# First MLP product: weight sums on DVE, each block loaded once for them, conv steps and stores at fixed distances

## The chip, the cores and the metric

The kernel runs on one core of a Trainium2 chip. The metric is the device time of one execution in microseconds; the median of three runs stands for a kernel. The engines are TensorE (PE in the profile; its weight loads are PEld), VectorE (DVE), ScalarE (ACT), GpSimd (POOL) and SyncE (SP). Each executes its own instructions in a fixed order and waits on semaphores. SP issues most transfers, POOL a few; both do so in the order of their queues.

## What is computed

One step of a hybrid decoder layer: a state-space and pooling mixer, attention over a memory, and a gated MLP with a causal width-3 convolution between its up-projection and its gate. The change concerns the MLP alone. For the 1024 prompt tokens and 8 samples of 4 tokens, 1056 in all, with D = 1024 and D_FF = 2816:

```python
h = rmsnorm(x, norm_ffn)
u = h @ w_up                                        # 1024 -> 2*2816
u, ffn_new = causal_dwconv(ffn_buf, u, ffn_conv_w, ffn_conv_b)   # width 3
g, val = jnp.split(u, [D_FF], axis=-1)
x = x + (jax.nn.silu(g) * val) @ w_down             # 2816 -> 1024
```

The convolution of each sample starts from two stored rows of its history, and the last two rows of each sequence are an output (ffn_new). The prompt starts from zeros.

## The kernel before

All arrays are held transposed: channels on the 128 partitions, the 1056 tokens along the free dimension. Every f32 operand of a product is split in two f32r parts: hi is a rounded copy made by ACT, lo is the rest, made by DVE as raw minus hi. A product is then three matmuls per block (hi x hi, lo x hi, hi x lo). Weight blocks are 128 x 512 (four 128 x 128 blocks, 256 KB): `wr` or `ws` is the raw tile, `wh` and `wl` the split ones. There are 3 buffers of wr, wh and wl each and 6 of ws.

The order of the program is written out by hand. `steps` is the list of weight steps; `prep()` does the next step and then issues what `issue` has for that step (loads, a few steps ahead). `next_unit()` runs `prep()` until two split blocks are ready and hands out the first, so that the split of the next block is written in front of the matmuls of this one. `tick()` is called inside the products: it runs hooks whose count is up (`later(n, fn)`: n ticks later) and advances background generators (`background(gen, every)`: one step of the generator each `every` ticks). The order in an engine's queue can still differ from the program's: the framework orders instructions that do not depend on each other, except where `strict` or `force` ties an engine to the program's order (line 92), and in the MLP neither is set.

The first MLP product is done by a seven-product scheme for 2 x 2 blocks. The blocks of one pair j (a gate block of 128 channels and its value block, 22 pairs) are a11, a12, a21, a22 (two output blocks by two halves of the contraction), the tokens are halved in lh and rh of 528. The seven weight operands are a11, a21 (replaced by a11 - a21), s2 = a11 - s1, a22, s1 = a21 + a22, a12, and s4 = s2 + a12; their products are called b11, t3, t2, t4, t1, b21 and b22. A product (`product`, line 1510) is 24 matmuls of 264 columns, in two PSUM banks, with four ticks. For 14 of the pairs, `EARLY`, b21 is made ahead of all pairs (`up_rh`) and put to scratch memory `m2`; for these pairs b11 goes to a tile q, and an accumulating load on POOL adds m2 to it.

`paired(j, names)` (line 228) sets up the weight steps of a pair. Its sums come about in two ways. s2 and a11 - a21 are made by DVE in the step `adds`. The other two are made by accumulating transfers on POOL (`more`): a21 is loaded a second time into a tile s1 and a22 is added to it on its way from memory; a12 is loaded into a tile s4 and s2 is added to it, from SBUF to SBUF. So a pair takes four loads of ws tiles and one of wr on SP, one more of wr for b21 (in the pair, or ahead for the EARLY ones), and two accumulating transfers on POOL.

`up(j)` (line 1541) makes the products of pair j. PSUM is evicted by ACT (b11, t3, t2, b22: 264 columns each half) or DVE with an addition (t4, t1, b21), into r0 and r1, the raw rows of the two blocks. The order of the products is b11 of j, b22 of j-1, then t3, t2, t4, t1 and, if j is not EARLY, b21 of j. `ends(s)` (line 1546) puts the history in front of the rows: POOL sets two columns to zero, copies the samples' history and, for the output, the last two rows; ACT copies the samples' 32 new columns behind their history. It is called right behind the product. `rest()` (line 1555) is the background generator that does the convolution: ACT scales and adds the bias, DVE does two multiply-adds (128 x 1104) per block, ACT the Silu of the gate, DVE the product of gate and value. Its steps go on every 1.3 ticks (`CONV_EVERY`), after 4 steps of delay per block (`REST_LAG`). Then DVE makes the operand sums of the second product (one for j < 11, three for j >= 11) and SP stores all to scratch memory `g1` or `g2`; the store is written right behind each result.

The second MLP product is a seven-product scheme too (`DN_ORDER`, line 1746 on). Its operands come back through `x_ops` (line 1643), a background generator: `fetch()` loads 264 KB from g1 or g2 into a q tile (4 buffers), and `parts` splits it in hi (ACT) and lo (DVE). Two loads are made at its start, and one more after every split, so that loads are two items ahead. It starts at pair 19 with one item, goes on in the last pair as `limit` allows, every 4 ticks (`X_EVERY_UP`), and in the second product every 3.6 ticks (`X_EVERY_DN`). `load_acc` loads the eight residual tiles that the second product adds to, one after each weight unit that does not begin a block, but not in the first block of b11.

Of the kernel before, what the change touches and what calls it, by code (L numbers as in the profile page):

```python
# [7 lines left out]
F32 = mybir.dt.float32  # L8
# [37 lines left out]
CONV_EVERY = 1.3  # L46
REST_LAG = 4
# [4 lines left out]
X_EVERY_DN = 3.6  # L52
SUMS_EVERY = 1.6
X_EVERY_UP = 4
# [24 lines left out]
def body(ctx, tc, A):  # L79
# [53 lines left out]
    ones = cst[:, 128:256]  # L133

# [93 lines left out]
    def paired(j, names):  # L228
        q, ids = {}, {}

        def get(n):
            load(ids[n])
            q[n] = raws[ids[n]][0]

        def more(n, x):
            load(ids[n])
            G.dma_start(raws[ids[n]][0], x() if callable(x) else x, accum_op=ALU.add)

        def adds():
            for n in ("a11", "a21", "s1"):  # L240
                get(n)
            q["s2"] = stmp()
            V.tensor_tensor(q["s2"], q["a11"], q["s1"], op=ALU.subtract)
            V.tensor_tensor(q["a21"], q["a11"], q["a21"], op=ALU.subtract)

        def one(n):
            if n not in q:
                get(n)
            wsplit(q[n], 512)

        n0 = len(steps) - 1
        steps.insert(n0, adds)
        for n, m, off, alloc in (("s1", "a21", -7, stmp), ("a11", "a11", -4, wtile), ("a21", "a21", -4, stmp),
                                 ("s4", "a12", 0, stmp), ("a22", "a22", 5, stmp)):
            ids[n] = source(up_part(j, m), n0, -off, alloc)
        for n, x, off in (("s1", up_part(j, "a22"), -5), ("s4", lambda: q["s2"], 1)):
            issue.setdefault(n0 + off, []).append(lambda n=n, x=x: more(n, x))
        if j:
            steps.insert(n0 + 1, lambda: one("a11"))
            names = names[1:]  # L260
        for n in names:
            if n == "a12":
                plains([up_part(j, "a12")])
            else:
                steps.append(lambda n=n: one(n))
# [1275 lines left out]
    def up(j):  # L1541
# [4 lines left out]
        def ends(s):  # L1546
            raw = raws2[s]
            ext = raw[:, 1058:1106].rearrange("p (b t) -> p b t", b=8)
            G.memset(raw[:, 0:2], 0.0)
            G.tensor_copy(ext[:, :, 0:2], fh[:, s])  # L1550
            S.activation(ext[:, :, 2:6], raw[:, 1026:1058].rearrange("p (b t) -> p b t", b=8), AF.Copy)
            G.tensor_copy(st[:, s, 0:2], raw[:, 1024:1026])
            G.tensor_copy(st[:, s, 2:18].rearrange("p (b t) -> p b t", b=8), ext[:, :, 4:6])

        def rest():
            for s in range(2):
                while len(done) <= s:
                    yield
                for _ in range(REST_LAG):
                    yield  # L1560
                raw, f = raws2[s], 2 * j + s
                c = cv[s] = utile()
                S.activation(c[:, :1104], raw[:, 2:1106], AF.Identity, scale=pc("fw", 3 * f + 2), bias=pc("fb", f))
                yield
                if s and j >= NH:
                    kept = stile()
                    dma(kept[:, :T], scr["g1"][j - NH][:, TH:])
                for q in range(2):
                    V.scalar_tensor_tensor(c[:, :1104], raw[:, q:q + 1104], pc("fw", 3 * f + q), c[:, :1104],
                                           op0=ALU.mult, op1=ALU.add)  # L1570
                    yield
                if s == 0:
                    S.activation(c[:, :1104], c[:, :1104], AF.Silu)
                    yield
# [4 lines left out]
            p = j % NH  # L1579
            yield  # L1580
            t = u[:, :TH]
            if j < NH:
                dma(scr["g1"][p][:, :T], g[:, :T])
                V.tensor_tensor(t, g[:, rh], g[:, lh], op=ALU.subtract)
                dma(scr["g1"][p][:, T:], t)
            else:
                dma(scr["g2"][p][:, :T], g[:, :T])
                V.tensor_tensor(kept[:, lh], g[:, rh], kept[:, lh], op=ALU.subtract)
                yield
                V.tensor_tensor(kept[:, rh], kept[:, rh], g[:, rh], op=ALU.subtract)  # L1590
                yield
                V.tensor_tensor(t, kept[:, rh], g[:, lh], op=ALU.add)
                dma(scr["g2"][p][:, T:2 * T], kept[:, :T])
                dma(scr["g2"][p][:, 2 * T:], t)
                stored.append(p)
# [18 lines left out]
        ends(0)  # L1614
        background(rest(), CONV_EVERY, bgs2)
# [10 lines left out]
        ends(1)  # L1626
        done.append(1)
        dma(A["o_ffn"][j], st)
# [12 lines left out]
    limit = [0]  # L1641

    def x_ops():
# [3 lines left out]
        def fetch():  # L1647
            if left:
                n, p = left.popleft()
                while n not in ("b11", "t1") and len(stored) <= p:  # L1650
                    next(bgs2[0][0])
# [5 lines left out]
        fetch()  # L1657
        fetch()
        for i, (n, p) in enumerate(todo):
            while i >= limit[0]:  # L1660
                yield
# [3 lines left out]
            fetch()  # L1665
# [23 lines left out]
    pace(X_EVERY_DN)  # L1689

# [56 lines left out]
    for i, name in enumerate(DN_ORDER):  # L1747
# [4 lines left out]
        for m, (c0, c1) in dn_units(name):  # L1752
# [15 lines left out]
            if c0 and len(acc) < 8 and (name, m) != ("b11", 0):  # L1768
# [217 lines left out]
```

## Time and profile before

| | us |
|---|---|
| runs | 1680.94, 1685.15, 1678.08 |
| median | 1680.94 |
| the profiled execution | 1682.67 |
| its span, first to last instruction | 1680.9 |
| first MLP product (b21 of the early pairs, then the pairs) | about 960 to 1440 in the span |
| second MLP product | about 1440 to 1675 |
| mean granted clock of TensorE | 0.997 of full speed |

A row of a group reads: line, engine, operation, what it writes from what it reads, its shapes, count, then busy time and the mean of one in ns, then the idle time of the engine just in front of these instructions and what ended it. In this kernel all instructions are recorded by one helper, so every row says L91, and groups are told apart by their tiles: wl<-ws,wh is the lo part of a weight block, ws<-wr,ws a sum of weight blocks, t<-t,par a conv step, t<-mb,t an eviction with addition, q<-scr_g an operand load of the second product. A row of a timeline has start, duration and, in brackets, the idle time before it with its releaser. In the table by stretches each engine has its busy time and count of instructions; PEclk is the granted clock of TensorE, 1.00 for full speed.

### The profile page before, as it was taken

How to read it: one execution, taken by the hardware profiler on the slowest of the kernel's cores; microseconds unless marked ns; L12 is line 12 of the kernel's file. 1: busy time of each engine (PE TensorE's matmuls, PEld its weight loads, DVE VectorE, ACT ScalarE, POOL GpSimd, SP SyncE). 2: the span in 40 equal slices, each digit the busy share in tenths (PEclk: the TensorE clock that was granted, in tenths of full speed). 3: DMA queues.
4: the chain of work that ended last, by engine and by line, in shares of the span. 5: the costliest groups of instructions: out<-in, count | busy, mean ns of one | idle time of the engine just before them, and what ended most of it. 6: DMA issues, size and time to landing. Idle time of an engine off the chain costs nothing. (4 is left out here: it accounts for less than half of the span.)

```text
span 1680.9 us, 30585 instructions
## 1 busy us (share of the span) xinstructions
PE 1642.8 (98%) x11808; PEld 1559.3 (93%) x11808; DVE 1180.9 (70%) x1999; ACT 784.4 (47%) x1402; POOL 138.7 (8%) x315
## 2 busy tenths in 40 slices
PE   9999999999999999999999999999999999999998
PEld 8899999899989889999878999999999989999997
DVE  6766768688679576654755896777777878776665
ACT  6565643444514343223533665555544545454451
POOL 0110000001000000000000002232122222100000
PEclk9999999999999999999999999999999999999999
DMA  6243354544696678853666756666566577896542
GB/s 219 85 160 87 66 134 105 111 87 107 224 314 230 192 252 304 301 165 105 233 226 192 228 182 170 177 167 180 145 167 199 168 205 218 284 302 203 159 139 103
DMA packets 187569, 306.57 MB, mean 182 GB/s; under 512 B 43920, under 2 KB 81296, under 8 KB 187424
## 3 DMA queue, kind: packets, MB, share of 16 engines
q1 hardware_dynamic: 178928, 289.04, 54.6%
q0 software_dynamic: 8496, 15.59, 5.6%
q8 instruction: 92, 1.51, 0.4%
q14 instruction: 53, 0.43, 0.1%
HBM read 221.26 MB, written 77.53 MB: 178 GB/s over the span
## 5 line engine op out<-in xcount | busy, mean ns | idle before, releaser
L91 PE MATMUL mb<-s,wh 128*128 128x264 f32 (+4 forms) x4800 | 908.3, 295 | 6.8 <-ACT wh L91 4.7
L91 PEld LDWEIGHTS mb<-s,wh 128*128 128x128 f32 x4800 | 759.5, 189 | 15.1 <-ACT wh L91 5.8
L91 PE MATMUL mb<-s,wl 128*128 128x264 f32 (+4 forms) x2400 | 667.5, 296 | 13.7 <-DVE wl L91 13.3
L91 PEld LDWEIGHTS mb<-s,wl 128*128 128x128 f32 x2400 | 445.8, 189 | 23.6 <-DVE wl L91 20.5
L91 ACT ACTIVATE wh<-wr 128x512 fp32r<-128x512 f32 (+1 forms) x298 | 184.7, 620 | 385.1 <-PE mb L91 177.2
L91 PE MATMUL mm<-s,wh 128*128 128x352 f32 x1728 | 340.9, 330 | 1.5 <-DVE s L91 1.5
L91 PEld LDWEIGHTS mm<-s,wh 128*128 128x128 f32 x1728 | 284.6, 188 | 7.9 <-DVE s L91 2.6
L91 DVE TENSOR_TENSOR wl<-wr,wh 128x512 fp32r<-128x512 f32 (+1 forms) x298 | 201.4, 677 | 109.9 <-ACT wh L91 107.4
L91 PE MATMUL mm<-s,wl 128*128 128x352 f32 x864 | 187.7, 324 | 0.0
L91 DVE SCALAR_TENSOR_TENSOR t<-t,par 128x1104 f32<-128x1104 f32 (+1 forms) x124 | 168.2, 1366 | 26.5 <-ACT t L91 25.4
L91 PEld LDWEIGHTS mm<-s,wl 128*128 128x128 f32 x864 | 147.2, 189 | 1.8 <-issue 1.2
L91 ACT ACTIVATE s<-s 128x512 f32<-128x512 f32 (+7 forms) x117 | 84.2, 730 | 94.2 <-DMA s<-scr_acs 60.7
L91 DVE TENSOR_TENSOR t<-t 128x1024 f32<-128x1024 f32 (+10 forms) x147 | 107.1, 731 | 14.8 <-DMA t<-w_dn 11.1
L91 ACT ACTIVATE wh<-ws 128x512 fp32r<-128x512 f32 x110 | 68.8, 626 | 63.0 <-DMA ws<-w_up 44.9
L91 DVE TENSOR_TENSOR s<-s 128x512 f32<-128x512 f32 (+8 forms) x90 | 74.4, 841 | 30.2 <-ACT s L91 29.8
L91 DVE TENSOR_TENSOR wl<-ws,wh 128x512 fp32r<-128x512 f32 x110 | 75.4, 686 | 21.3 <-ACT wh L91 20.4
L91 ACT ACTIVATE t<-t 128x32 f32<-128x32 f32 (+2 forms) x87 | 46.8, 537 | 88.2 <-DVE t L91 87.7
L91 DVE TENSOR_TENSOR s<-mb,s 128x264 f32<-128x264 f32 (+6 forms) x140 | 61.0, 473 | 30.9 <-PE mb L91 14.9
L91 DVE TENSOR_TENSOR s<-q,s 128x528 fp32r<-128x528 f32 x81 | 56.6, 705 | 36.1 <-ACT s L91 35.7
L91 ACT ACTIVATE t<-t,par 128x1104 f32<-128x1104 f32 (+1 forms) x56 | 73.2, 1307 | 15.5 <-DVE t L91 11.6
L91 ACT ACTIVATE s<-q 128x528 fp32r<-128x528 f32 x81 | 51.9, 643 | 53.7 <-DMA q<-scr_g 50.6
L91 DVE TENSOR_TENSOR ws<-wr,ws 128x512 f32<-128x512 f32 x44 | 30.2, 691 | 57.4 <-issue 31.5
(192 smaller groups left out, 1506.1 us busy)
## 6 DMA issues: line engine op xcount, KB each, us to landing
ws<-w_up SPq DMA_DIRECT2D x88, 256.0 KB, 3.6
q<-scr_g SPq DMA_DIRECT2D x77, 264.0 KB, 3.8
wr<-w_in SPq DMA_DIRECT2D x56, 256.0 KB, 2.9
wr<-w_mo SPq DMA_DIRECT2D x46, 256.0 KB, 3.0
scr_g<-t SPq DMA_DIRECT2D x22, 528.0 KB, 5.2
wr<-w_up SPq DMA_DIRECT2D x44, 256.0 KB, 3.2
s<-scr_acs SPq DMA_DIRECT2D x33, 256.0 KB, 5.1
t<-w_dn SPq DMA_DIRECT2D x32, 256.0 KB, 4.5
```

The source lines that it names most:

```text
L91: i = fn(*args, **kwargs)
```

## The change

Sums: `more` goes. a21, a22 and a11 are loaded three to four steps ahead of the sums, a12 three steps behind their first step. DVE makes all four: a11 - a21 in the step `adds`, then s1 in place of a21, s2, and, five steps on (`SUM_LAG`), s4 in place of s2, whose own split comes before that. b21 of a pair that is not EARLY splits the same a12 tile. Per pair four loads on SP are left, two of ws and two of wr.

History: `ends` is all on ACT, and it is called in `rest`, two steps behind the product. The prompt's zeros come from a small tile `nil`.

Conv steps: `rest` goes on at every tick, with pauses of 2, 1, 2 and 2 ticks (`PAUSE`): in front of `ends`, behind it, in front of each multiply-add, and in front of the product of gate and value. The Silu of the gate follows the second multiply-add in the same tick.

Stores: each is written three ticks (`STORE_LAG`) behind its result, with `later`. The store of the history output goes to POOL's queue.

Operand loads: in the first MLP product one load is out at a time (`depth`), in the second two; an item takes two steps of the generator, one that loads and one that splits, at half the former distance. The next load is issued in the step behind the split. `load_acc` is called only behind the second weight unit of each block.

```diff
-CONV_EVERY = 1.3
-REST_LAG = 4
+PAUSE = (2, 1, 2, 2)
+STORE_LAG = 3
+SUM_LAG = 5
...
-X_EVERY_DN = 3.6
+X_EVERY_DN = 1.8
 SUMS_EVERY = 1.6
-X_EVERY_UP = 4
+X_EVERY_UP = 2
...
+    nil = cp.tile([P, 2], F32, name="nil")
+    nc.vector.memset(nil, 0.0)
...
             load(ids[n])
             q[n] = raws[ids[n]][0]
 
-        def more(n, x):
-            load(ids[n])
-            G.dma_start(raws[ids[n]][0], x() if callable(x) else x, accum_op=ALU.add)
-
         def adds():
-            for n in ("a11", "a21", "s1"):
+            for n in ("a11", "a21"):
                 get(n)
+            q["s3"] = stmp()
+            V.tensor_tensor(q["s3"], q["a11"], q["a21"], op=ALU.subtract)
+
+        def first():
+            get("a22")
+            q["s1"] = q["a21"]
+            V.tensor_tensor(q["s1"], q["a21"], q["a22"], op=ALU.add)
+
+        def second():
             q["s2"] = stmp()
             V.tensor_tensor(q["s2"], q["a11"], q["s1"], op=ALU.subtract)
-            V.tensor_tensor(q["a21"], q["a11"], q["a21"], op=ALU.subtract)
 
         def one(n):
-            if n not in q:
-                get(n)
             wsplit(q[n], 512)
+
+        def fourth():
+            V.tensor_tensor(q["s2"], q["s2"], q["a12"], op=ALU.add)
 
         n0 = len(steps) - 1
         steps.insert(n0, adds)
-        for n, m, off, alloc in (("s1", "a21", -7, stmp), ("a11", "a11", -4, wtile), ("a21", "a21", -4, stmp),
-                                 ("s4", "a12", 0, stmp), ("a22", "a22", 5, stmp)):
-            ids[n] = source(up_part(j, m), n0, -off, alloc)
-        for n, x, off in (("s1", up_part(j, "a22"), -5), ("s4", lambda: q["s2"], 1)):
-            issue.setdefault(n0 + off, []).append(lambda n=n, x=x: more(n, x))
+        for n, off, alloc in (("a21", -4, stmp), ("a22", -4, stmp), ("a11", -3, wtile), ("a12", 3, wtile)):
+            ids[n] = source(up_part(j, n), n0, -off, alloc)
+        issue.setdefault(n0 + 1, []).append(first)
+        issue.setdefault(n0 + 2, []).append(second)
+        issue.setdefault(n0 + SUM_LAG, []).append(lambda: (get("a12"), fourth()))
         if j:
             steps.insert(n0 + 1, lambda: one("a11"))
             names = names[1:]
         for n in names:
-            if n == "a12":
-                plains([up_part(j, "a12")])
-            else:
-                steps.append(lambda n=n: one(n))
+            steps.append(lambda n=n: one({"s4": "s2", "a21": "s3"}.get(n, n)))
 
     def down_weights(name, m, c):
         kind = {"t3": 0, "b22": 1, "t1": 2, "t2": 3}
...
         def ends(s):
             raw = raws2[s]
             ext = raw[:, 1058:1106].rearrange("p (b t) -> p b t", b=8)
-            G.memset(raw[:, 0:2], 0.0)
-            G.tensor_copy(ext[:, :, 0:2], fh[:, s])
+            S.activation(raw[:, 0:2], nil, AF.Copy)
+            S.activation(ext[:, :, 0:2], fh[:, s], AF.Copy)
             S.activation(ext[:, :, 2:6], raw[:, 1026:1058].rearrange("p (b t) -> p b t", b=8), AF.Copy)
-            G.tensor_copy(st[:, s, 0:2], raw[:, 1024:1026])
-            G.tensor_copy(st[:, s, 2:18].rearrange("p (b t) -> p b t", b=8), ext[:, :, 4:6])
+            S.activation(st[:, s, 0:2], raw[:, 1024:1026], AF.Copy)
+            S.activation(st[:, s, 2:18].rearrange("p (b t) -> p b t", b=8), raw[:, 1026:1058].rearrange("p (b t) -> p b t", b=8)[:, :, 2:4], AF.Copy)
 
         def rest():
             for s in range(2):
                 while len(done) <= s:
                     yield
-                for _ in range(REST_LAG):
+                for _ in range(PAUSE[0]):
+                    yield
+                ends(s)
+                for _ in range(PAUSE[1]):
                     yield
                 raw, f = raws2[s], 2 * j + s
                 c = cv[s] = utile()
                 S.activation(c[:, :1104], raw[:, 2:1106], AF.Identity, scale=pc("fw", 3 * f + 2), bias=pc("fb", f))
-                yield
-                if s and j >= NH:
-                    kept = stile()
-                    dma(kept[:, :T], scr["g1"][j - NH][:, TH:])
+                if s:
+                    later(STORE_LAG, lambda: G.dma_start(A["o_ffn"][j], st))
+                    if j >= NH:
+                        kept = stile()
+                        dma(kept[:, :T], scr["g1"][j - NH][:, TH:])
                 for q in range(2):
+                    for _ in range(PAUSE[2]):
+                        yield
                     V.scalar_tensor_tensor(c[:, :1104], raw[:, q:q + 1104], pc("fw", 3 * f + q), c[:, :1104],
                                            op0=ALU.mult, op1=ALU.add)
-                    yield
                 if s == 0:
                     S.activation(c[:, :1104], c[:, :1104], AF.Silu)
-                    yield
+            for _ in range(PAUSE[3]):
+                yield
             g, u = cv[0], cv[1]
             V.tensor_tensor(g[:, :TP], g[:, :TP], u[:, :TP], op=ALU.mult)
             gs, us = [x[:, 1058:1106].rearrange("p (b t) -> p b t", b=8)[:, :, 0:4] for x in (g, u)]
             V.tensor_tensor(g[:, TP:T].rearrange("p (b t) -> p b t", b=8), gs, us, op=ALU.mult)
             p = j % NH
-            yield
             t = u[:, :TH]
+            yield
             if j < NH:
-                dma(scr["g1"][p][:, :T], g[:, :T])
+                later(STORE_LAG, lambda: dma(scr["g1"][p][:, :T], g[:, :T]))
                 V.tensor_tensor(t, g[:, rh], g[:, lh], op=ALU.subtract)
-                dma(scr["g1"][p][:, T:], t)
+                later(STORE_LAG, lambda: dma(scr["g1"][p][:, T:], t))
             else:
-                dma(scr["g2"][p][:, :T], g[:, :T])
+                later(STORE_LAG, lambda: dma(scr["g2"][p][:, :T], g[:, :T]))
                 V.tensor_tensor(kept[:, lh], g[:, rh], kept[:, lh], op=ALU.subtract)
                 yield
                 V.tensor_tensor(kept[:, rh], kept[:, rh], g[:, rh], op=ALU.subtract)
+                later(STORE_LAG, lambda: dma(scr["g2"][p][:, T:2 * T], kept[:, :T]))
                 yield
                 V.tensor_tensor(t, kept[:, rh], g[:, lh], op=ALU.add)
-                dma(scr["g2"][p][:, T:2 * T], kept[:, :T])
-                dma(scr["g2"][p][:, 2 * T:], t)
-                stored.append(p)
+
+                def last_store():
+                    dma(scr["g2"][p][:, 2 * T:], t)
+                    stored.append(p)
+
+                later(STORE_LAG, last_store)
             yield
 
         q = qp.tile([P, TH], F32, tag="q", name="q")
...
         product("t1", pa, r0[:, e0], r0[:, e0])
         if j == NJ - 1:
             limit[0] = NH
-        ends(0)
-        background(rest(), CONV_EVERY, bgs2)
+        background(rest(), 1, bgs2)
         done.append(0)
         raws2[1] = r1 = utile()
         if j not in EARLY:
...
             limit[0] = 2 * NH
         if j in EARLY:
             S.activation(r1[:, e1], q, AF.Copy)
-        ends(1)
         done.append(1)
-        dma(A["o_ffn"][j], st)
 
     nt = [0]
 
...
     xd = {n: [] for n in xparts}
     todo = [(n, p) for n in (*DN_ORDER, "b21") for p in range(NH)]
     stored = []
-    limit = [0]
+    limit, depth = [0], [1]
 
     def x_ops():
         coming = deque()
...
         def fetch():
             if left:
                 n, p = left.popleft()
-                while n not in ("b11", "t1") and len(stored) <= p:
-                    next(bgs2[0][0])
+                assert n in ("b11", "t1") or len(stored) > p
                 t, i = xparts[n]
                 r = qp.tile([P, TH], F32, tag="q", name="q")
                 dma(r, scr[t][p][:, i * TH:(i + 1) * TH])
                 coming.append(r)
 
-        fetch()
-        fetch()
         for i, (n, p) in enumerate(todo):
             while i >= limit[0]:
+                yield
+            while left and len(coming) < depth[0]:
+                fetch()
                 yield
             x = stile(F32R)
             parts(x[:, lh], x[:, rh], coming.popleft())
             xd[n].append(x)
-            fetch()
             yield
 
     acc = []
...
         last = g
     next(last, 0)
     pace(X_EVERY_DN)
+    depth[0] = 2
 
 
 
...
                                   start=(first and k == 0 and pi == 0), stop=(k == NH - 1 and pi == 2),
                                   skip_group_check=not first)
                 tick()
-            if c0 and len(acc) < 8 and (name, m) != ("b11", 0):
+            if c0 == DN_CUTS[1][0] and len(acc) < 8:
                 load_acc()
             if c1 == NH * P:
                 evict(name, m, ps)
```

More of the change, by code (lines that the diff above doesn't have):

```diff
@@ L1579, in rest @@
             p = j % NH
+            t = u[:, :TH]
             yield
-            t = u[:, :TH]
             if j < NH:
-                dma(scr["g1"][p][:, :T], g[:, :T])
+                later(STORE_LAG, lambda: dma(scr["g1"][p][:, :T], g[:, :T]))
                 V.tensor_tensor(t, g[:, rh], g[:, lh], op=ALU.subtract)
-                dma(scr["g1"][p][:, T:], t)
+                later(STORE_LAG, lambda: dma(scr["g1"][p][:, T:], t))
             else:
-                dma(scr["g2"][p][:, :T], g[:, :T])
+                later(STORE_LAG, lambda: dma(scr["g2"][p][:, :T], g[:, :T]))
                 V.tensor_tensor(kept[:, lh], g[:, rh], kept[:, lh], op=ALU.subtract)
```

## The prediction

> **What bounds the kernel now.** I read the first line of the page, then the busy time of the engines by stretches of the span, then the groups of instructions in one stretch, and last the timelines of single stops.
>
> ```profile
> span 1680.9 us, 30585 instructions
> ```
>
> ```profile
> core 0: us, PE busy (x) PEld busy (x) DVE busy (x) ACT busy (x) POOL busy (x), PEclk, DMA share, GB/s
> 1004.00:1080.00 76.00, 75.22 (x612) 74.68 (x611) 53.41 (x78) 42.34 (x85) 19.58 (x45) 1.00 0.71 180
> 1080.00:1180.00 100.00, 95.18 (x761) 93.17 (x761) 71.60 (x100) 54.18 (x104) 27.27 (x58) 1.00 0.65 171
> 1180.00:1280.00 100.00, 96.78 (x781) 95.42 (x781) 73.47 (x106) 51.52 (x101) 21.08 (x54) 1.00 0.60 168
> 1280.00:1380.00 100.00, 97.92 (x781) 95.66 (x780) 74.71 (x110) 48.04 (x96) 25.88 (x50) 1.00 0.67 183
> 1380.00:1392.00 12.00, 9.23 (x52) 8.72 (x51) 10.29 (x14) 8.30 (x15) 1.75 (x2) 0.72 0.64 206
> 1392.00:1440.00 48.00, 48.00 (x396) 48.00 (x395) 42.30 (x65) 29.00 (x56) 12.67 (x22) 1.00 0.78 237
> 1440.00:1520.00 80.00, 76.66 (x618) 75.36 (x617) 54.43 (x93) 39.06 (x67) 2.40 (x1) 1.00 0.88 297
> ```
>
> TensorE is the bound. The change touches 1004 to 1440 us, the main part of the first MLP product (22 channel pairs, six or seven weight products each), and by its operand loads the first part of the second product behind it. It takes no matmul away, so all that it can win is time in which TensorE stands. From 1392 to 1440 TensorE never stands: 396 matmuls in 48.0 us, 0.121 us each, which is the pace to hold the rest against; a weight product of 24 matmuls takes 2.91 us. Over 1004 to 1440 the PE column adds up to 422.3 of 436 us: 13.7 us idle. A stop costs a little more than its idle time: a matmul lasts 0.28 us and the next normally starts after 0.12 us, so 0.16 us is to be added. The weight-load groups, whose waits hold this part too, give the total:
>
> ```profile
> L91 PEld LDWEIGHTS mb<-s,wh 128*128 128x128 f32 x2246 | 350.6, 189 | 5.5 <-ACT t L91 3.3 <-ACT wh L91 2.1
> ...
> L91 PEld LDWEIGHTS mb<-s,wl 128*128 128x128 f32 x1125 | 213.0, 189 | 14.9 <-DVE wl L91 14.7
> ...
> L91 ACT ACTIVATE wh<-ws 128x512 fp32r<-128x512 f32 x110 | 68.8, 626 | 63.0 <-DMA ws<-w_up 44.9 <-PE mb L91 15.9 <-issue 2.3
> ...
> L91 DVE TENSOR_TENSOR ws<-wr,ws 128x512 f32<-128x512 f32 x42 | 28.9, 691 | 57.4 <-issue 31.5 <-DMA ws<-w_up 25.2
> ...
> L91 ACT ACTIVATE t<-t 128x1104 f32<-128x1104 f32 x21 | 23.7, 1127 | 23.1 <-DVE t L91 23.1
> ...
> L91 ACT ACTIVATE t<-t 128x32 f32<-128x32 f32 x44 | 10.2, 231 | 57.2 <-DVE t L91 56.7
> ```
>
> The last field of a row is idle time in front of its instructions. Weight loads waited 5.5 + 14.9 = 20.4 us, nearly all for the split of a weight block, wl on DVE above all. In the PE timeline I count 31 stops in this stretch and, idle time plus restart, 19.5 us. They have three causes.
>
> First, late sums. DVE's sums of weight blocks had 57.4 us of idle time ahead of them, and ACT's splits of such blocks 44.9 us waiting for their loads. One case, on three engines (POOL, DVE, PE):
>
> ```profile
> 1094.16 0.86 POOL L91 DMA_DIRECT2D ws<-w_up  x1 [2.58 <-DVE t L91]
> ```
>
> ```profile
> 1096.61 0.68 DVE L91 TENSOR_TENSOR wl<-ws,wh 128x512 fp32r<-128x512 f32 x1
> 1102.93 0.69 DVE L91 TENSOR_TENSOR ws<-wr,ws 128x512 f32<-128x512 f32 x1 [5.63 <-issue]
> 1103.54 0.69 DVE L91 TENSOR_TENSOR wl<-ws,wh 128x512 fp32r<-128x512 f32 x1
> ```
>
> ```profile
> 1104.28 0.39 PE L91 MATMUL mb<-s,wl 128*128 128x264 f32 x1 [0.80 <-DVE wl L91]
> ```
>
> The accumulating load of one block onto another goes out on POOL at 1094.16. DVE has nothing ahead of the sum that needs it, stands 5.63 us, and the split for the product that runs now is queued behind that sum: TensorE stands 0.80 us, a stop of 0.96 us. The profile names no releaser, but the sum reads the accumulated block. I put 17 stops and 11.3 us to this kind: those where a sum, or the split of a block loaded for or accumulated into a sum, came out of a wait. The first and the last of them:
>
> ```profile
> 1016.33 0.39 PE L91 MATMUL mb<-s,wh 128*128 128x264 f32 x1 [0.49 <-ACT t L91]
> ```
>
> ```profile
> 1364.25 0.39 PE L91 MATMUL mb<-s,wh 128*128 128x264 f32 x1 [0.91 <-ACT t L91]
> ```
>
> Second, crowding on DVE without any wait: conv steps stand so close that a split comes late.
>
> ```profile
> 1165.64 1.36 DVE L91 SCALAR_TENSOR_TENSOR t<-t,par 128x1104 f32<-128x1104 f32 x1
> 1167.11 1.23 DVE L91 TENSOR_TENSOR t<-t 128x1024 f32<-128x1024 f32 x1
> 1168.25 0.43 DVE L91 TENSOR_TENSOR t<-mb,t 128x264 f32<-128x264 f32 x1
> 1168.60 0.68 DVE L91 TENSOR_TENSOR wl<-wr,wh 128x512 fp32r<-128x512 f32 x1
> ```
>
> ```profile
> 1169.33 0.39 PE L91 MATMUL mb<-s,wl 128*128 128x264 f32 x1 [0.26 <-DVE wl L91]
> ```
>
> Eleven stops are of this kind, 4.6 us together, 0.42 us each.
>
> Third, one event: the operand loads for the second product begin, three at once in front of weight loads on SP's queue.
>
> ```profile
> 1375.56 1.57 SPq L91 DMA_DIRECT2D q<-scr_g  x3
> 1377.24 1.72 SPq L91 DMA_DIRECT2D ws<-w_up  x2
> ```
>
> ```profile
> 1384.74 0.50 PE L91 MATMUL mb<-s,wh 128*128 128x264 f32 x1 [1.85 <-ACT wh L91]
> 1386.16 0.59 PE L91 MATMUL mb<-s,wl 128*128 128x264 f32 x1 [0.92 <-DVE wl L91]
> ```
>
> These stops make 3.6 us (19.5 - 11.3 - 4.6). The row 1380 to 1392 above shows a granted clock of 0.72 and 52 matmuls in 12 us; at the pace of 0.121 they need 6.3 us, so 5.7 us are lost there, 3.6 in stops and 2.1 by the clock.
>
> **The change part by part.** *Sums and loads.* For each pair two accumulating transfers go (42 sums of 22 pairs are in the stretch, two each; the two transfers per pair were on POOL) and a21, a22 and a12 are loaded for the sums once (the 14 early pairs still load a12 again for the product made ahead). DVE gets two more sums per pair: 44 x 0.691 = 30.4 us. DVE was busy 325.8 of 436 us, 75%; it comes to 356 us, 82%, or 84% of a stretch that is 12 us shorter. No sum waits for an accumulation any more, and a22 is loaded four steps ahead of them, where the program before has its load at its own split. The sums still wait for plain loads, issued three or four steps ahead:
>
> ```profile
> ws<-w_up SPq DMA_DIRECT2D x84, 256.0 KB, 3.7
> ...
> ws<-w_up POOLq DMA_DIRECT2D x21, 256.0 KB, 5.3
> ```
>
> 3.7 us against 5.3, and with no first load that must land before the second starts. Bounds: all of the 11.3 us goes, or only 3 us if sums still stand early in DVE's order and meet a late load. DVE's order before has a sum about two products ahead of its use (the one at 1102.93), so I do not take all: -8.5 us, three quarters. The accumulation of the early products onto q stays on POOL.
>
> *History copies.* Four POOL operations per channel half become ACT copies: 176 x 0.231 = 40.7 us. ACT was busy 233.4 of 436 us, 54%, and comes to 63%. Against that, the copy that ACT made right behind the eviction waited 56.7 us for DVE, with weight splits behind it on ACT; two steps later DVE has mostly finished. Bounds -2 us (a few stops go with that wait) to +4 us (eight copies, 1.8 us per pair, fall in front of a split now and then); I take 0: ACT's idle 46% hides the copies, and the two effects pull opposite ways.
>
> *Conv steps.* One step at each tick (a quarter of a product, 0.73 us), with two ticks between two 1.37 us operations of DVE. With the added sums, crowding (4.6 us) may go or grow: from -4.6 us (all gone) to +10 us (one stop of 0.42 us more per pair, 22 x 0.42 = 9.2). I take +1.5, nearer to the present row, because spacing and added work pull opposite ways.
>
> *Stores and queues.* The stores of g1 and g2 go to SP three ticks after the result; SP no longer waits for DVE there with weight loads behind it. The store of the conv history moves to POOL's queue, where only the 15 accumulations onto q come behind it. I give it 0 by itself: it is what lets the plain loads be early, and if it does not, the third rival below has the price.
>
> *Operand loads.* At their start one load instead of three goes out, though the load of the kept half stays. Bounds -5.7 to 0; I take -5. In the second product the lead shrinks: a load used to go out two items ahead, 7.2 ticks, now it goes half an item later, 5.4 ticks, 3.9 us.
>
> ```profile
> L91 ACT ACTIVATE s<-q 128x528 fp32r<-128x528 f32 x37 | 23.7, 643 | 34.9 <-DMA q<-scr_g 34.8
> ```
>
> ACT already waits 34.8 us for such loads between 1440 and 1520, and that stretch has 3.3 us of idle PE. Bounds: -3 (the loads of the accumulator are spread out, and stores are lagged) to +4 (the idle time doubles); I take 0.
>
> The clock term rests on this trace: stops of 2.0 and 1.3 us, close together, and then a granted clock of 0.72. [...]
>
> Sum: -8.5 + 1.5 - 5 = -12 us. The profiled execution took 1682.67 us for its span of 1680.9, so it would come to 1670.7; it lies 1.7 us over the median of the runs, 1680.94, so the median comes to 1668.9: **1669 us**.
>
> **The rivals.** *DVE gives it back.* If one more 0.42 us stop per pair follows from the added sums, 9.2 us, and the waits for sums and the start of the operand loads go as above (-13.5), 4.3 us are left: 1676.6, no difference that can be measured. For it: the wl splits are what PE waits for, 14.7 of 20.4 us, and DVE gets the work. Against it: DVE has 57.4 us of waiting to give for 30.4 us of sums.
>
> *A Silu in front of the splits; slower.* The Silu now stands in the same tick as the second conv operation, with no step between. If ACT's order puts it ahead of an eviction and the next wh, the chain behind that conv operation is 1.13 (Silu) + 0.38 (eviction) + 0.63 (wh) + 0.69 (wl) = 2.83 us, against 2.91 us of one product. It decides from the point where the conv operation ends later than 0.1 us after the product in whose last tick it stands. With 1.37 us for that operation a stop of about 1.3 us per pair follows: 22 x 1.3 = 28.6, less 13.5: 1696. For it: ACT already waited 23.1 us for 21 Silus, 1.1 us each. Against it: those waits show hardly a stop before, and the order of the engines' queues is not plainly the program's (the sum at 1102.93), so the split may stand first.
>
> *The loads do not come early.* If SP is as late as before and sums stand as early, the plain loads win only 3 us, the event 5: -8 + 1.5 = -6.5, 1674.4.
>
> **How the numbers follow.** A measurement of this kernel tells 0.5%, 8.4 us, from no change. Forecast and its neighbourhood 0.58; DVE gives it back 0.14; loads not early 0.14; Silu 0.14. Best ends: -11.3 - 4.6 - 5.7 - 3 = -24.6, 1656. The range goes from there up to 1686, which takes in both middle cases and the milder part of the Silu case. The likeliest case's own range is 1656 to 1677. Faster than 1672.5: nearly all of the forecast's share and a third of the loads' case, 0.6. Within: 0.25, most of the two middle cases. Slower: 0.15, the Silu case and little else.
>
> **What would show it.** Right: no idle time of several us in front of DVE's sums; PE idle between 1004 and about 1430 at 5 to 7 us instead of 13.7; no stretch at a clock under 1 near the start of the operand loads; DVE at 82 to 85% there. The DVE rival shows as more stops of 0.3 to 0.6 us with DVE busy in front; the Silu rival as stops of over 1 us, one per pair, with the Silu in front of wh on ACT; the loads' case as idle time on sums released by plain loads. Wrong: more PE idle in the second product than before, or stops where no trace of before has any.

## The result, and the profile after

The changed kernel takes 1659.49 us (median of five runs), the kernel before 1681.77 on the same chip: the ratio is 0.987, with a 95% interval of 0.986 to 0.989, or 22 us less. The prediction had 1669, from 1656 to 1686.

The profiled execution took 1659.16 us, its span 1657.3. The table by stretches of the changed kernel (columns as in the table of before; the pairs now run from 1004 to about 1418):

```profile
960.00:1004.00 44.00, 41.92 (x334) 41.28 (x333) 39.94 (x72) 28.78 (x66) 0.00 (x0) 0.98 0.53 167
1004.00:1080.00 76.00, 76.00 (x618) 76.00 (x618) 60.90 (x89) 46.88 (x114) 5.51 (x8) 0.99 0.52 147
1080.00:1180.00 100.00, 100.00 (x821) 100.00 (x820) 86.87 (x121) 64.02 (x165) 8.50 (x12) 1.00 0.47 129
1180.00:1280.00 100.00, 100.00 (x821) 100.00 (x820) 87.08 (x125) 58.74 (x144) 4.50 (x7) 1.00 0.44 138
1280.00:1380.00 100.00, 100.00 (x821) 100.00 (x820) 89.69 (x131) 59.77 (x149) 5.94 (x9) 1.00 0.45 146
1380.00:1425.00 45.00, 45.00 (x370) 45.00 (x370) 40.82 (x59) 30.63 (x68) 1.09 (x2) 1.00 0.76 250
```

From 1004 on TensorE does not stand at all in the pairs: 421 of 421 us, where 13.7 of 436 were idle. 821 matmuls in 100 us, against 761 to 781, are 0.122 us each. DVE is busier, 365 of 421 us or 87%; between 1080 and 1380 us the DMA share has gone from 0.64 to 0.45.

The groups of instructions of the changed kernel between 1004 and 1425 us:

```profile
L92 PEld LDWEIGHTS mb<-s,wl 128*128 128x128 f32 x1148 | 216.5, 189 | 0.0
...
L92 DVE TENSOR_TENSOR ws<-wr,ws 128x512 f32<-128x512 f32 x43 | 29.8, 692 | 1.3
...
L92 DVE TENSOR_TENSOR ws<-ws,wr 128x512 f32<-128x512 f32 x22 | 15.2, 692 | 0.7
L92 DVE TENSOR_TENSOR ws<-ws 128x512 f32<-128x512 f32 x21 | 14.4, 687 | 1.6 <-DMA ws<-w_up 1.4
...
L92 ACT ACTIVATE t<-t 128x32 f32<-128x32 f32 x44 | 10.0, 226 | 6.5 <-DVE t L92 6.1
...
L92 ACT ACTIVATE fst<-t 128x16 f32<-128x16 f32 x44 | 9.0, 204 | 0.0
```

The sums are now twice as many, and 3.6 us (1.3 + 0.7 + 1.6) of idle time stand in front of all of them, where 57.4 stood. ACT's copy of the new columns waits 6.5 us instead of 57.2, and a history copy takes 0.20 us. The DVE timeline of the changed kernel, with sums and conv steps:

```profile
1165.56 0.69 DVE L92 TENSOR_TENSOR ws<-wr,ws 128x512 f32<-128x512 f32 x1
1166.17 1.36 DVE L92 SCALAR_TENSOR_TENSOR t<-t,par 128x1104 f32<-128x1104 f32 x1
1167.45 0.68 DVE L92 TENSOR_TENSOR ws<-ws 128x512 f32<-128x512 f32 x1
1168.05 1.36 DVE L92 SCALAR_TENSOR_TENSOR t<-t,par 128x1104 f32<-128x1104 f32 x1
1169.33 0.68 DVE L92 TENSOR_TENSOR wl<-ws,wh 128x512 fp32r<-128x512 f32 x1
```

No bracket stands in these rows: DVE has no idle time between them. Two sums and two conv steps stand in the 3.8 us ahead of a split, and PE does not stand.

One stop is left, in the last products that are made ahead of the pairs (there are 15 of them; `EARLY` is range(11) and four more, so the 14 of the description is wrong). ACT and PE:

```profile
1000.62 0.63 ACT L92 ACTIVATE wh<-wr 128x512 fp32r<-128x512 f32 x1 [1.51 <-DMA wr<-w_up]
```

```profile
1001.31 0.52 PE L92 MATMUL mb<-s,wh 128*128 128x264 f32 x2 [1.98 <-ACT wh L92]
```

ACT's split waited there for the load of an early a12 block, and a half clock of 3.4 us came behind it (0.50 from 1002.12 to 1005.54; 0.98 and 0.99 in the first two rows of the table).

The two traces have the same matmuls in the same order, so they can be set against each other matmul by matmul. From number 6580 to 9960, the pairs and the last of the products ahead of them, the kernel before needs 438.4 us and the changed one 416.7: 21.7 us less. Below, "in the pairs" means these numbers. The 640 matmuls after them, the first part of the second product, take 83.0 and 80.5 us. Ahead of them the two executions differ by 0.7 us. Over all the profiled executions below, though, that first part, in which their programs hardly differ, takes from 994 to 1004 us; so parts are compared, not whole spans.

### The profile page after: what moved, and what is told of

Same layout as the page of the kernel before. It is cut to its first block, busy times and chain, and to the rows that moved or that the text cites. A ratio compares the mean times of both kernels' runs of the same rounds, so it can differ in the third digit from the quotient of the medians.

```text
span 1657.3 us, 30394 instructions
## 1 busy us (share of the span) xinstructions
PE 1633.0 (99%) x11808; PEld 1556.8 (94%) x11808; DVE 1213.8 (73%) x2044; ACT 805.2 (49%) x1578; POOL 51.5 (3%) x117
## 4 chain that ended last, share of the span: by engine, by line
PE 74%; DMA 6%; DVE 4%; ACT 1%; issue 1%; SPq 0%; DVEq 0%; ACTq 0%
PE mb L92 59%; PE mm L92 12%; PE ms L92 3%; DMA s<-scr_acs 2%; DVE s L92 2%; DMA q<-scr_g 1%; DVE wl L92 1%; ACT s L92 1%; DMA wr<-w_mk 1%; DMA wr<-w_mo 1%; DVE t L92 0%; DMA scr_pool<-t 0%; DMA ld<-scr_pool 0%; ACT wh L92 0%; DMA wr<-w_up 0%
## 5 line engine op out<-in xcount | busy, mean ns | idle before, releaser
L92 ACT ACTIVATE s<-s 128x512 f32<-128x512 f32 (+7 forms) x117 | 84.2, 731 | 93.4 <-DMA s<-scr_acs 57.4
L92 DVE TENSOR_TENSOR wl<-ws,wh 128x512 fp32r<-128x512 f32 x110 | 75.7, 689 | 22.0 <-ACT wh L92 21.7
L92 ACT ACTIVATE t<-mb 128x264 f32<-128x264 f32 (+1 forms) x136 | 53.3, 393 | 57.4 <-PE mb L92 50.3
L92 PE MATMUL mb<-s 128*128 128x256 f32 (+2 forms) x414 | 68.8, 323 | 0.0
```

Of the source, the lines that this page charges most:

```text
L92: i = fn(*args, **kwargs)
```

## The experiments

Each of the three groups shared its runs of the kernel before, and the chips differ a little (1688 and 1683 us for the kernel before), so ratios to it are compared: the changed kernel has 0.987.

**The sums alone.** The kernel before with the new `paired`:

```diff
-        for n, x, off in (("s1", up_part(j, "a22"), -5), ("s4", lambda: q["s2"], 1)):
-            issue.setdefault(n0 + off, []).append(lambda n=n, x=x: more(n, x))
+        issue.setdefault(n0 + 1, []).append(first)
+        issue.setdefault(n0 + 2, []).append(second)
+        issue.setdefault(n0 + SUM_LAG, []).append(lambda: (get("a12"), fourth()))
```

> The kernel before with the new weight sums alone: all four sums on DVE, blocks loaded once for them; history, conv steps, stores and operand loads as before. If the late sums are the cause (17 stops, 11.3 us), they go and the crowding on DVE keeps its 4.6 us or grows by some: 1668 to 1673 against 1681 before. If the distances of the conv steps and the history copies bring the gain, the added DVE work has nowhere to go and the time is 1679 to 1690.

Measured: 0.991 (0.988 to 0.994). Its pairs have four stops instead of 32, 5.7 instead of 20.4 us (a stop here is a matmul that starts over 0.25 us after the one before it, and its cost what is over 0.121 us; the 31 stops and 19.5 us of the prediction are the same count from 1004 us on). The stops of the crowded kind are gone too, though the conv steps stand at their old distances. The first stop is the one at the early a12 load; the other large one waits for an accumulating load, that of m2 onto q (POOL, ACT and PE of this kernel):

```profile
1387.22 5.60 POOL L92 COPY fst<-t 128x16 f32<-128x16 f32 x1
1392.77 0.86 POOL L92 DMA_DIRECT2D q<-scr_m  x1
```

```profile
1398.16 0.64 ACT L92 ACTIVATE t<-q 128x528 f32<-128x528 f32 x1 [5.93 <-DMA q<-scr_m]
```

```profile
1399.39 0.59 PE L92 MATMUL mb<-s,wh 128*128 128x264 f32 x1 [2.91 <-ACT t L92]
```

ACT's copy of q waits 5.93 us, with an eviction and a weight split behind it, and a half clock of 6.8 us comes again. It is not the stop of the kernel before: that one is at matmul 9570, this one at 9750, over seven products later, and at 9570 there is none now. POOL issues this load only behind a history copy, at matmul 9721; in the kernels below whose history copies are on ACT or two ticks later it goes out at 9674 to 9676, and none of them stops there.

**The sums of before.** The changed kernel with the old `paired`, the reverse edit.

> The changed kernel with the sums of before: two accumulating transfers per pair on POOL, a21 loaded twice. If the late sums are the cause: 1669 to 1674 against 1659.5, with stops of about 1 us behind sums that waited. If the distances and the history copies are the cause, it stays at 1658 to 1663, since DVE then has 30 us less to do.

Measured: 0.995 (0.993 to 0.997), 20 stops and 13.5 us in the pairs. So the sums are worth about 0.8% of the time with the rest of the change, and the rest about 0.5% with the old sums: the event at the operand loads does not come, and stops of the crowded kind, nine of them, cost 1.8 us instead of 4.6. A stop of this kernel, DVE and PE:

```profile
1104.47 0.68 DVE L92 TENSOR_TENSOR wl<-ws,wh 128x512 fp32r<-128x512 f32 x1
1110.28 0.69 DVE L92 TENSOR_TENSOR ws<-wr,ws 128x512 f32<-128x512 f32 x1 [5.13 <-issue]
1110.89 2.77 DVE L92 SCALAR_TENSOR_TENSOR t<-t,par 128x1104 f32<-128x1104 f32 x2
1113.57 0.69 DVE L92 TENSOR_TENSOR wl<-ws,wh 128x512 fp32r<-128x512 f32 x1
```

```profile
1114.32 0.40 PE L92 MATMUL mb<-s,wl 128*128 128x264 f32 x1 [2.28 <-DVE wl L92]
```

DVE stands 5.13 us at the sum, and then has two conv steps to do ahead of the split that PE needs: the work that the wait held up comes in one piece. The trace of before has the same ahead of the stop at 1169.33, which the prediction took for crowding without any wait:

```profile
1158.66 0.69 DVE L91 TENSOR_TENSOR ws<-wr,ws 128x512 f32<-128x512 f32 x1 [4.55 <-issue]
1159.27 0.69 DVE L91 TENSOR_TENSOR wl<-ws,wh 128x512 fp32r<-128x512 f32 x1
1159.99 0.69 DVE L91 TENSOR_TENSOR ws<-wr,ws 128x512 f32<-128x512 f32 x1
```

From there to the late split, for 10 us, DVE has 0.1 us of idle time. Six of the eleven crowded stops come 10.7 us behind a sum that waited 4.5 to 5.9 us, with no more idle time than that between.

**Program order on DVE.** The sum at 1102.93 of the kernel before stands about two products ahead of its use. To see whether that place is the harm, DVE is tied to the program's order in the pairs:

```diff
     xg = x_ops()
+    V.force = True
     for j in range(NJ):
...
+    V.force = False
     pace(X_EVERY_DN)
```

> The kernel before with DVE's instructions in the order of the program while the pairs are made; nothing else is changed. If a late transfer harms because a sum stands in DVE's queue about two products ahead of its use, in front of splits that PE needs sooner, the sums move behind those splits and most of the 11.3 us goes: 1668 to 1675. If the transfers are late for any order, or the order itself costs as much: 1679 or more.

Measured: 1.018 (1.016 to 1.020), slower. The groups of this kernel, 1004 to 1470 us:

```profile
L91 PEld LDWEIGHTS mb<-s,wl 128*128 128x128 f32 x1128 | 215.3, 191 | 32.7 <-DVE wl L91 32.4
...
L91 ACT ACTIVATE wh<-ws 128x512 fp32r<-128x512 f32 x110 | 68.7, 628 | 91.0 <-DMA ws<-w_up 37.6 <-DVE ws L91 29.7 <-PE mb L91 23.5
...
L91 DVE TENSOR_TENSOR ws<-wr,ws 128x512 f32<-128x512 f32 x42 | 27.0, 683 | 0.0
```

The sums no longer wait (0.0 against 57.4), but now ACT's splits wait for the sums, 29.7 us, and still for loads, 37.6. The sums behind the splits cost more, so my theory that their place is the harm finds no support. It is not refuted either: the edit ties all of DVE's instructions, conv steps and evictions too, and not the sums alone.

**The history on POOL again** (place as in the changed kernel):

```diff
-            S.activation(raw[:, 0:2], nil, AF.Copy)
-            S.activation(ext[:, :, 0:2], fh[:, s], AF.Copy)
+            G.memset(raw[:, 0:2], 0.0)
+            G.tensor_copy(ext[:, :, 0:2], fh[:, s])
...
-            S.activation(st[:, s, 0:2], raw[:, 1024:1026], AF.Copy)
+            G.tensor_copy(st[:, s, 0:2], raw[:, 1024:1026])
```

> The changed kernel with the history's zeros, copies and output rows on POOL again (ACT keeps the one copy it had), at the new place two ticks behind the product. By the prediction the copies cost and bring nothing: 1658 to 1662. If ACT's or DVE's waits for POOL were part of the loss: 1664 or more.

Measured: 0.985 (0.983 to 0.988), one stop in the pairs. The engine of these copies makes no difference here, with the rest of the change in place.

**The old pace of the conv steps**, with the copies right behind the product:

```diff
-        background(rest(), 1, bgs2)
+        ends(0)
+        background(rest(), 1.3, bgs2)
...
-                for _ in range(PAUSE[0]):
+                for _ in range(4):
```

> The changed kernel with the conv steps paced as before (a step every 1.3 ticks, four steps of delay, one step between two DVE operations) and the history copies, on ACT, right behind the product. If the distances remove the crowding, it comes back: 4 to 10 us, 1664 to 1670, with stops of about 0.4 us and DVE busy ahead of them. If the crowding went with the late sums: 1658 to 1662.

Measured: 0.985 (0.982 to 0.988), one stop of 1.5 us in the pairs. With the new sums the distances bring nothing either. Crowding needed the late sums; with the old sums the rest of the change made it smaller.

**The old operand loads.**

```diff
+        fetch()
+        fetch()
         for i, (n, p) in enumerate(todo):
...
-            while left and len(coming) < depth[0]:
-                fetch()
-                yield
...
+            fetch()
             yield
```

> The changed kernel with the operand loads of before: two out at the start, a third behind the first split, one step per item. If the three loads made the event at the start of the operand loads (3.6 us of stops and 2.1 by the clock): 1663 to 1666 on the scale of 1659.5, with stops and a half clock where they start. If the event came from the late accumulations around it: 1658 to 1662; the second product could win up to 2 us by the longer lead.

Measured: 0.985 (0.983 to 0.988); one stop in the pairs, the early one, and no slow clock at the start of the operand loads. In this company the three loads do no harm. On the kernel before, with the new sums, the new operand loads:

> The kernel before with the new weight sums and the new operand loads; history, conv steps and stores as before. The sums alone gave 0.991 and left one event of 3 us and a half clock at the start of the operand loads, where an accumulating load onto q was late. If the operand loads bring that transfer late: the event goes, 0.987 to 0.988, the whole gain of the change. If not, 0.990 to 0.992 as with the sums alone.

Measured: 0.990 (0.988 to 0.992), not to be told from 0.991 with the sums alone by the times. In the profile the 2.91 us of idle time behind q are 1.38 us and no half clock comes there, so the pairs take 416.7 us, as long as in the changed kernel; but later, in the second product, stops of 5.3 us and one half clock do. What part of the smaller stop is the loads' is not settled.

**Stores right behind the results**, the history output on SP:

```diff
-                later(STORE_LAG, lambda: dma(scr["g1"][p][:, :T], g[:, :T]))
+                dma(scr["g1"][p][:, :T], g[:, :T])
```

and so for all of them.

> The changed kernel with every store right behind its result and the history output on SP. If the lag brings the plain loads early: sums wait for plain loads, 1662 to 1670. If SP has time enough: 1658 to 1662, by the prediction's zero.

Measured: 0.988 (0.984 to 0.991), no difference by the times, and one stop in the pairs. In the first part of the second product it has 5.2 us of stops and a half clock, 85.1 us for the 640 matmuls against 80.5. The two other kernels that combine the new sums with stores that do not lag have 84.4 and 85.5 there, all other kernels 79.1 to 83.0. So the lag may be worth some 4 us behind the pairs, and nothing in them; the times do not confirm that.

**More work on DVE.** Two or four additions per pair without use, on a raw tile that is done with:

```diff
+            V.tensor_tensor(raws2[0][:, 2:514], raws2[0][:, 2:514], raws2[0][:, 514:1026], op=ALU.add)
             g, u = cv[0], cv[1]
```

> The changed kernel with two more 128x512 additions on DVE per pair, without use, on a raw tile that is done with, ahead of the product of gate and value: 44 x 0.69 = 30.4 us. DVE goes from 87 to 94% in the pairs. If DVE is near its end, as the rival that gives the gain back has it: 9 to 30 us more. If waits, not work, made the stops: no more than 2 us.

> As the one before with four additions per pair, 60.8 us more on DVE, which would be over 100% of the pairs' time by busy time, or about 97% if each operation holds up the next one 0.08 us less than its duration. By either theory the time rises: 10 to 40 us more than 1659.5. Under 5 us would mean that DVE had more room than the busy rows say.

Measured: 0.987 (0.984 to 0.990) and 0.988 (0.985 to 0.990): 60 us of added work, at this place, do not show within 0.3%. The stretches of the kernel with four more:

```profile
1080.00:1180.00 100.00, 100.00 (x820) 100.00 (x820) 95.73 (x140) 66.63 (x169) 8.62 (x12) 1.00 0.47 132
1180.00:1280.00 100.00, 100.00 (x821) 100.00 (x820) 96.97 (x150) 58.65 (x144) 4.51 (x7) 1.00 0.44 138
1280.00:1380.00 100.00, 100.00 (x821) 100.00 (x821) 98.00 (x149) 59.77 (x147) 5.05 (x8) 1.00 0.47 152
```

DVE is busy for 96 to 98% of the time, and PE still never stands in these 300 us; one stop of 1.3 us comes at 1414, beside the early one. For two additions the case of waits, not work, held; for four, where both theories had a cost, the expectation was wrong.

**A better kernel.** The early a12 blocks go to the ws buffers, idle at that time, four steps ahead:

```diff
-    plains(up_part(j, "a12") for j in EARLY)
+    for j in EARLY:
+        i = source(up_part(j, "a12"), len(steps), 4, stmp)
+        steps.append(lambda i=i: plain(i))
```

> The changed kernel; the a12 blocks of the early products go to ws tiles (6 buffers, idle then), loaded four steps ahead instead of two. The one stop that is left in the pairs, 2.1 us and 3.4 us of half clock behind it, waits for such a load: 2 to 4 us less than the changed kernel, 0.985 to 0.986. If the stop is DVE's crowding there, no difference, 0.987.

Measured: 0.985 (0.983 to 0.986), 1657.63 us. The stop at 1001.31 is 0.51 us of idle time now:

```profile
998.32 0.39 PE L92 MATMUL mb<-s,wl 128*128 128x264 f32 x1 [0.51 <-DVE wl L92]
```

What is left waits for DVE, no longer for a load, and there is no half clock. The pairs take 413.9 us, 2.8 less than in the changed kernel. But with the early loads of the changed kernel the pairs take 414.5 to 415.7 us in the runs with the history on POOL, with the old pace, with stores that do not lag and with two more additions, and no half clock came there; so the stop itself is worth about 1 us, and the rest came with the half clock: 3.4 us at 0.50 are 1.7 us lost, by an estimate. The interval of the ratio touches that of the changed kernel: the times do not tell the two apart. With three operand loads out (`depth[0] = 3`) as well:

> As the one before, and three operand loads out at a time in the second product instead of two (4 q tiles). Four stops, 2.1 us, are left there, behind operands that came late: up to 2 us less than the one before, 0.984 to 0.985. If the loads are late for the traffic and not for the lead, no difference or more stops.

Measured: 0.985 (0.984 to 0.986), three stops and 1.7 us in the first part of the second product instead of four and 2.8: nothing that can be measured.

## Why the prediction was right, and where it fell short

The bound was right, and so was the path: TensorE is the bound (busy for 422.3 of 436 us before, for 421 of 421 after), its stops in the pairs were the gain to be had, and DVE, standing at late sums, made most of them. The sign and the range held. What the sums waited for was read wrongly, and the size was 12 us forecast, 22 measured; three terms of the sum were set too low.

- *Late sums, -8.5.* All of the 11.3 us went, but not for the reason given. The step "the sum reads the accumulated block", for the sum at 1102.93, failed. These are the transfers onto ws that POOL issued at 1094.16 and SP at 1096.04, in the kernel before:

```profile
ws<-w_up POOLq DMA_DIRECT2D x1, 256.0 KB, 5.4
```

```profile
ws<-w_up SPq DMA_DIRECT2D x1, 256.0 KB, 6.8
```

  The accumulating load had landed at 1099.55, 3.4 us ahead of the sum; the plain one landed at 1102.85, 0.08 us ahead of it. So it is with 15 of the 16 sums that waited over 1 us: each starts 0.02 to 0.12 us behind the landing of a plain load of SP that took from 4.2 to 7 us. In the changed kernel with the sums of before it is 15 of 16 again. Plain loads were thus late already, the case that the prediction held back a quarter for, and the term came right in part by luck: the change takes these waits away too. For 19 of the last 21 pairs a21, the first of a pair's two loads onto ws, goes out 7.5 us or more ahead of its sum, where before DVE was free for the sum at 1102.93 already 1.3 us behind the issue; and the loads land in a median of 2.8 us, not 3.7:

```profile
ws<-w_up SPq DMA_DIRECT2D x42, 256.0 KB, 2.8
```

  The sums of the changed kernel wait 1.4 us in all for loads. What made the plain loads late, the traffic of the accumulations and of the second load of a21 or their place in SP's order, no run separates.

- *Crowding, +1.5.* It was -4.6, all of it. The step that failed is the one that took eleven stops "without any wait" as a cause of their own. In the kernel with the sums alone they are gone at the old distances, so they needed the late sums; for six of them the trace of before has the wait, 10.7 us ahead: DVE worked off what a late sum had held up.
- *The event at the operand loads, -5.* The whole 5.7 us went. The trace of before bears the reading out, ACT stood there for an operand load:

```profile
1380.09 0.65 ACT L91 ACTIVATE s<-q 128x528 fp32r<-128x528 f32 x1 [5.03 <-DMA q<-scr_g]
```

  But the three loads alone do not make it: with the new sums they bring no stop there, neither in the kernel before nor in the changed one. Nor does it come with the old sums and one load at a time, in the run with the sums of before. It needed both, so the term cannot be credited to the operand loads alone.
- *History copies 0, stores 0.* Both hold by the times, taken one by one. The copies cost 0.19 to 0.21 us each, less than the 0.231 of the bound. Left as they were beside the new sums, on POOL right behind the product, they stand ahead of the accumulating load that ACT waits 5.93 us for in the run with the sums alone.
- *Operand loads in the second product, 0.* 2.5 us were won there in the profiles, inside its bounds of -3 to +4; but kernels with the same operand loads and lagged stores differ by as much, 79.1 to 82.8 us, so the zero stands as far as can be told.
- New, and in no term: the stop in the early products became longer, a price of the new sums. Its idle time is 0.75 us in all three kernels with the old sums and 1.15 to 2.58 us in the nine with the new ones and the early a12 blocks in wr. In the changed kernel it costs 2.1 us, with 3.4 us of half clock behind it, where 0.9 us, and 0.4 at the next stop, were. On the other side, delays too short to be counted as stops, 32 of them outside the half clock, cost 3.3 us before and 0.1 us after.

DVE did not give it back: the argument against that rival, that DVE has more waiting to give than the sums cost, was right, and there was room beyond it, as the runs with 30 and 60 us more show. The Silu rival did not come in: ACT waited 7.4 us for 22 Silus, instead of 23.1 us for 21. The loads that do not come early did not come in either. The clock term held: the half clock went with the stops, and where the row 1380 to 1392 of before has 0.72, the row 1380 to 1425 of the changed kernel has 1.00.

## What to carry to other kernels

An engine's busy share said little here on whether it holds up the others: between 1080 and 1380 us TensorE stopped 25 times with DVE busy for 73% of the time, and not once with DVE at 97%. What counts is whether an instruction in its queue waits for something late, because all behind it wait too and then come in one piece (two conv steps and a split behind the sum that stood 5.13 us, with the sums of before); so look at the idle time ahead of each group first, and count the crowded stops that follow such a wait to the wait. Where the profile names no releaser, compare the start of the instruction with the landings of all the loads it reads; the one that is easiest to suspect need not be the last. A sum made on the way of a transfer was not free here: two additions of 0.69 us on a busy engine were better than two accumulating transfers, of 5.3 and 4.0 us in the median, and the second load of a block that they need.

## What the runs showed of the hardware

- An accumulating load of 256 KB from memory landed in a median of 5.3 us in the kernel before (21 of them, 1004 to 1440 us), a plain one onto ws in 3.7 (84); in the changed kernel, without these accumulations, plain ones took 2.8 (42, 1004 to 1425 us).
- In these traces the granted clock fell to half behind some stops and not behind others. In the kernel before it was 0.50 for 6.83 us from 1384.86 on, when the stop with 1.85 us of idle PE had just ended and the one of 0.92 us had not begun, so the first was enough there; in the changed kernel for 3.41 us from 1002.12 on, behind a single stop with 1.98 us of idle PE; with the sums alone for 6.8 us, behind one of 2.91 us. It stayed at 1.00 behind 1.55 us at 222.30 and 1.52 us at 302.77 in the kernel before and behind 1.72 us at 951.82 in the changed one, and no half clock came behind the 2.28 us in the kernel with the sums of before. What sets these stops apart was not shown.
- Consecutive DVE instructions of the changed kernel, in the timeline from 1165.56 to 1169.33, start about 0.08 us before the one ahead has ended by its row (0.61 us apart at a duration of 0.69), so 88 added sums of 0.69 us, 60.7 us by their rows, would take 53.7 us of its time, by an estimate from these two numbers.
